# A decoder trunk with split fp32 weights: another order of the work between its two layers, and two other reckoned times in its planner

## The chip, the cores and the metric

The kernel runs on one core of a Trainium2 chip. The metric is device time in microseconds (us), lower is better. The engines are called as the profile calls them: PE (TensorE, the matrix engine), ACT (ScalarE), DVE (VectorE), POOL (GpSimd) and SP (SyncE, which here only issues transfers).

## The reference

`h` has 256 tokens of 1024 features in fp32. Two layers each do

```python
h = h + 0.5 * swiglu(rmsnorm(h, ffn1_norm), ffn1_w_gate, ffn1_w_up, ffn1_w_down)   # D_FF = 2752
u = rmsnorm(h, mix_norm); z = u @ w_in        # gated mLSTM and sliding-window attention
h = h + 0.5 * (sigmoid(gA) * (A @ W_A) + sigmoid(gB) * (B @ W_B)) @ w_out
h = h + 0.5 * swiglu(rmsnorm(h, ffn2_norm), ffn2_w_gate, ffn2_w_up, ffn2_w_down)
h = h + sigmoid(rmsnorm(h, ple_norm) @ ple_gate_w) * (p[i] @ ple_proj_w)           # p[i]: 256 x 256
```

`rmsnorm` needs the whole row of a token, so nothing of a block's first matmul can start for a token before the block ahead has finished that token.

## The kernel before, in words

**Tiles and parts.** The 256 tokens are two token tiles of 128, t0 and t1 (`NT` = 2). Every fp32 weight W is split into a rounded high half `wh` and a rest `wl`, and activations likewise, so each product is three matmuls (`mm3`): x-high by `wh`, x-high by `wl`, x-low by `wh`. Weights come from HBM into one of two 1 MB buffers `raw`; each holds two parts of 128 x 1024. A part is split by a cast on ACT (`wh<-raw`) and a subtraction on DVE (`wl<-raw,wh`). The split parts go into a ring of eight. A `raw` buffer can be loaded again when the `wl` of its second part is done.

**The planner.** All work is written out in one program by a planner that keeps a reckoned time for each engine (class `Clock`); the engines then run their instructions in the order written. Before each pair of matmul groups `tick` advances chains of work whose reckoned time has come, and calls `feed`, which splits the next part if the reckoned times of ACT, DVE and of the part's arrival allow it. `Clock.DMA` is a fixed latency and a time per MB, from which `load` reckons arrivals. `store` counts parts split and not yet used; with `haste` set, `feed` splits no further part once `store` has reached `HASTE` = 3, so that DVE and ACT are free for the norm at a block's end. If a matmul needs a part that isn't split, `need` splits it then and there.

**The end of a block.** `project` runs a matmul over eight parts (two units n = 0, 1 of four parts) for both token tiles. With `first` = 3 and `last` = 5 the first three parts run for t0, then for t1, and the last five for t0, then for t1, so t0 ends 30 matmuls before t1. When an accumulator (n, t) is complete, `use` is deferred as a chain: in `ple` it is a tanh on ACT (`sg<-pg`), a DVE operation with `pp` (`sg<-sg,pp`), and `then`, which adds to `h` on DVE, takes the sum of squares on ACT (`sq<-h`) and, at n = 1, starts `norm`: `ms` on DVE, a power `r` on POOL, two `xn` on DVE, eight transposes on PE (`tp<-ident,xn`), and their copies `uT` (high on ACT, low on DVE). `haste` is set in `project` at the item `hurry` and cleared when t0's `norm` has issued its transposes.

**The blocks** are, per layer, ffn1, mix, ffn2, ple. A feed-forward block begins with `by_token`, whose matmuls the trace calls `gu`; in layer 1's ffn1 the first six parts run for t0 (36 matmuls) and then for t1. Its product `sg<-sg,gu` on DVE is transposed on PE (`tp<-ident,sg`). Further columns are `pg` and `pu`, the output `dn`. In `ple` the gate's matmul is `pg` too.

**The embeddings.** `prelude` of `ple` runs when ffn2's `dn` begins: SP issues the load of `p`, and `later_T` lets the planner place the transposes `tp<-ident,p` at a reckoned 5.0 us later. Their results are used by `pp`, after all of `dn`.

Of the kernel before, what the change touches and what calls it, by code (L numbers as in the profile page):

```python
# [22 lines left out]
NT = T // P  # L23
KT = D // P
DEPTH = 2
# [10 lines left out]
STORE, HASTE = 4, 3  # L36
# [9 lines left out]
def half(n):  # L46
    return slice(n * NB, (n + 1) * NB)


class Part:  # L50


    def __init__(self, c0, k, n):
        self.c0, self.k, self.n = c0, k, n
        self.hi = self.lo = self.ready = None
        self.fresh = True
        self.rows = None


class Clock:  # L60
# [5 lines left out]
    SYNC = 0.1  # L66
    TABLE = 1.4
    SETS = {AF.Silu: {0}, AF.Exp: {1}, AF.Tanh: {0, 1}, AF.Ln: {2}}
    DMA = (1.0, 2.9)

    def __init__(self):
        self.t = dict.fromkeys(self.COST, 0.0)
# [34 lines left out]
    def load(self, ready, mb=1.0):  # L107

        latency, per = self.DMA
        self.dma = max(self.dma, ready, self.now) + mb * per  # L110
# [53 lines left out]
class Trunk:  # L164
# [7 lines left out]
    def __init__(self, ctx, tc, a, out):  # L172
        self.tc, self.a, self.out = tc, a, out
        self.clock = Clock()
        self.nc = Core(self.clock, tc.nc)
        pool = lambda name, bufs, **k: ctx.enter_context(tc.tile_pool(name=name, bufs=bufs, **k))
        self.const = pool("const", 1)
        self.rawp = pool("raw", RAW)
        self.wp = pool("w", RING)
        self.slots = pool("slots", 22)  # L180
        self.gp = pool("g", 1)
        self.sc = pool("sc", 7)
        self.small = pool("small", 6)
        self.psum = pool("psum", 8, space=PSUM)
        self.n = 0
        self.jobs, self.bg, self.haste, self.entry = [], [], False, None
        self.pending, self.loaded, self.store = deque(), deque(), 0
        self.free, self.raws = deque([0.0] * RING), deque([0.0] * RAW)
        self.consts()
# [138 lines left out]
    def feed(self, must=False):  # L328

        clock = self.clock  # L330
        if not self.loaded or not self.free:
            return
        raw, parts = self.loaded[0]
        part, arrival = parts[0]
        slack = AHEAD[self.store >= STORE]
        if not must and max(self.free[0], arrival, clock.t["scalar"] - slack, clock.t["vector"] - slack) > clock.now:
            return
        if not must and self.haste and self.store >= HASTE:
            return
        self.store += 1  # L340
        ready = max(self.free.popleft(), arrival)
        parts.popleft()
        last = not parts
        if last:
            self.loaded.popleft()
        w = part.k * part.n
        hi = self.wp.tile([P, QU], F32R, tag="wh", name=self.name("wh"))[:, :w]
        lo = self.wp.tile([P, QU], F32R, tag="wl", name=self.name("wl"))[:, :w]

        def chain():  # L350
            src = raw[:, part.c0 : part.c0 + w]
            if part.rows is None:
                yield from self.splitting(hi, lo, src)
            else:
                self.tc.nc.gpsimd.memset(lo[part.rows.stop :].bitcast(F32), 0.0)
                self.nc.scalar.copy(hi, src)
                yield
                r = part.rows
                self.nc.vector.tensor_tensor(lo[r], src[r], hi[r].bitcast(F32), op=ALU.subtract)
            part.ready = clock.done()  # L360
            if last:
                self.raws.append(part.ready)
                self.prefetch()

        part.hi, part.lo = (x.rearrange("p (k n) -> p k n", k=part.k) for x in (hi, lo))
        part.chain = self.later(chain())
        self.entry = self.entry or part.chain
        outer = clock.begin(dma=ready)
        self.advance(part.chain)
        clock.end(outer)  # L370
# [20 lines left out]
        mm(ps, xh, wl, start=False, stop=False, **kw)  # L391
        mm(ps, xl, wh, start=False, stop=stop, **kw)

    def project(self, units, xT, base, use, first=0, last=0):


        units = [[(sum(q.k for q in unit[:i]), part) for i, part in enumerate(unit)] for unit in units]
        todo = [(n, k0, part) for n, unit in enumerate(units) for k0, part in unit]
        cut = len(todo) - last
        apart = lambda items: [(x, t) for t in range(NT) for x in items]  # L400
        order = apart(todo[:first]) + [(x, t) for x in todo[first:cut] for t in range(NT)] + apart(todo[cut:])
        hurry = order[-last - 1] if last else None
        uses = {id(part): NT for _, _, part in todo}
        ps = {}
        for (n, k0, part), t in order:
            if ((n, k0, part), t) == hurry:
                self.haste = True
            if k0 == 0:
                ps[n, t] = None
            tok = slice(t * P, (t + 1) * P)  # L410
            for k in range(part.k):
                kk = k0 + k
                self.tick()
                xT.wait(kk, t)
                self.need(part)
                if ps[n, t] is None:
                    ps[n, t] = self.bank(base)[:, : part.n]
                self.mm3(ps[n, t], xT[0](kk, tok), xT[1](kk, tok), part.hi[:, k, :], part.lo[:, k, :], kk == 0,
                         kk == KT - 1)
            uses[id(part)] -= 1  # L420
            if not uses[id(part)]:
                self.drop(part)
            if kk == KT - 1:
                self.defer(use, n, t, ps[n, t])
# [94 lines left out]
    def norm(self, t, ss, g, xT):  # L519

        nc = self.nc
        ms, r = self.col("ms"), self.col("r")
        nc.vector.scalar_tensor_tensor(ms, ss[:, 0:1], EPS, ss[:, 1:2], op0=ALU.add, op1=ALU.add)
        self.power(r, ms)
        yield
        xn = []
        for n in range(2):
            xn.append(self.scr("xn"))
            nc.vector.scalar_tensor_tensor(xn[n], self.h[t][:, half(n)], r, g[n], op0=ALU.mult, op1=ALU.mult)
        yield  # L530
        for n in range(2):
            self.to_T(xn[n], xT, n * 4, t)
        if t == 0:
            self.haste = False

    def first_norm(self, t, g, xT):

        ss = self.col("ss", 2)
        for n in range(2):
            self.sumsq(t, n, ss)  # L540
        yield
        norm = self.norm(t, ss, g, xT)
        yield next(norm)
        yield next(norm)
        if t == 0 and self.entry is not None:
            self.advance(self.entry)
        yield from norm
# [133 lines left out]
    def ple(self, l, xT, sink):  # L681


        nc, a = self.nc, self.a
        prepare, then = sink
        pT = self.new_T("pT", 2)
        pp = []
        wp = self.columns(a["ple_proj_w"][l].rearrange("(k p) n -> p k n", p=P))
        wg = self.pair(a["ple_gate_w"][l], 0)

        def run():
            prepare()
            ps = {(t, n): self.bank("pp") for t in range(NT) for n in range(2)}
            for k in range(2):
                for t in range(NT):
                    self.tick()
                    self.need(wp[k])
                    pT.wait(k, t)
                    tok = slice(t * P, (t + 1) * P)
                    for n in range(2):  # L700
                        s = half(n)
                        self.mm3(ps[t, n], pT[0](k, tok), pT[1](k, tok), wp[k].hi[:, 0, s], wp[k].lo[:, 0, s],
                                 k == 0, k == 1)
                self.drop(wp[k])
            for t in range(NT):
                pp.append(self.slot("pp"))
                for n in range(2):
                    nc.scalar.copy(pp[t][:, n * NB : (n + 1) * NB], ps[t, n])

            def use(n, t, ps):  # L710
                sg = self.scr("sg")
                nc.scalar.activation(sg, ps, AF.Tanh, scale=0.5)
                nc.vector.scalar_tensor_tensor(sg, sg, 1.0, pp[t][:, n * NB : (n + 1) * NB], op0=ALU.add, op1=ALU.mult)
                then(n, t, sg)
            self.project(wg, xT, "pg", use, first=3, last=5)
        self.jobs.append(run)

        def prelude():
            p = self.slot("p")[:, : NT * 2 * P].rearrange("p (t n) -> p t n", t=NT)
            nc.sync.dma_start(p, a["p"][l, 0].rearrange("(t p) n -> p t n", p=P))  # L720
            for t in range(NT):
                self.later_T(p[:, t, :], pT, 0, t, 2, self.clock.now + 5.0)
        return prelude


# [552 lines left out]
```

## Time and profile before

| | |
|---|---|
| median of 3 runs | 1404.9 us (1402.35 to 1405.91) |
| the profiled execution | 1401.73 us |
| its span in the profile | 1400.0 us |
| PE busy | 1384.3 us (99%) |
| DVE, ACT busy | 863.0 us (62%), 727.8 us (52%) |
| transfers | 243.81 MB, mean 174 GB/s |

The profile shows one execution; the span runs from its first to its last instruction. "Busy" counts a PE at half its clock as busy too, so the windows view, which gives the granted clock (PEclk, 1.00 is full), is needed beside it. Nearly all instructions are issued in one helper, line L130, so groups are told apart by the names of their operands. L324 is the load of a `raw`, L498 that of a norm's gain, L720 that of `p`.

### The profile page before, as it was taken

How to read it: one execution, taken by the hardware profiler on the slowest of the kernel's cores; microseconds unless marked ns; L12 is line 12 of the kernel's file. 1: busy time of each engine (PE TensorE's matmuls, PEld its weight loads, DVE VectorE, ACT ScalarE, POOL GpSimd, SP SyncE). 2: the span in 40 equal slices, each digit the busy share in tenths (PEclk: the TensorE clock that was granted, in tenths of full speed). 3: DMA queues.
4: the chain of work that ended last, by engine and by line, in shares of the span. 5: the costliest groups of instructions: out<-in, count | busy, mean ns of one | idle time of the engine just before them, and what ended most of it. 6: DMA issues, size and time to landing. Idle time of an engine off the chain costs nothing.

```text
span 1400.0 us, 21954 instructions
## 1 busy us (share of the span) xinstructions
PE 1384.3 (99%) x9056; PEld 1249.0 (89%) x9056; DVE 863.0 (62%) x1213; ACT 727.8 (52%) x1138; POOL 53.8 (4%) x84
## 2 busy tenths in 40 slices
PE   8999999999999999999999999999999999999998
PEld 6999887899899889988879998878998998999886
DVE  5655457656886665454565554586668876554544
ACT  5554346765665454443554443467656654444433
POOL 0000012000000000000000000120000000000000
PEclk9999999999999999999999999999999999999999
DMA  6665645355545565565456566443545544755651
GB/s 210 221 206 172 219 147 182 107 135 169 177 151 181 166 204 188 166 232 181 149 172 210 178 198 212 143 145 117 151 151 196 175 158 161 220 190 182 203 180 60
DMA packets 125830, 243.81 MB, mean 174 GB/s; under 512 B 14977, under 2 KB 23841, under 8 KB 125730
## 3 DMA queue, kind: packets, MB, share of 16 engines
q1 hardware_dynamic: 125730, 242.41, 54.2%
q8 instruction: 71, 1.16, 0.3%
q14 instruction: 29, 0.24, 0.1%
HBM read 241.34 MB, written 1.05 MB: 173 GB/s over the span
## 4 chain that ended last, share of the span: by engine, by line
PE 93%; DMA 3%; DVE 2%; ACT 1%; issue 1%; POOL 0%; SPq 0%; ACTq 0%; POOLq 0%
PE dn L130 16%; PE pg L130 15%; PE pu L130 14%; PE gt L130 7%; PE z L130 7%; PE gu L130 6%; PE kvq L130 5%; PE ya L130 3%; PE v L130 3%; PE ym L130 3%; PE og L130 3%; PE yo L130 3%; PE tp L130 3%; PE sc L130 2%; DMA raw<-in_ffn_w_gate_dram 1%; PE ha L130 1%
## 5 line engine op out<-in xcount | busy, mean ns | idle before, releaser
L130 DVE TENSOR_TENSOR wl<-raw,wh 128x1024 fp32r<-128x1024 f32 (+1 forms) x448 | 541.5, 1222 | 372.8 <-ACT wh L130 369.3
L130 ACT CAST wh<-raw 128x1024 fp32r<-128x1024 f32 x448 | 461.8, 1049 | 432.7 <-PE dn L130 88.4
L130 PE MATMUL dn<-wh,hid 128*128 128x512 f32 x688 | 217.9, 395 | 0.0
L130 PE MATMUL pg<-uT,wh 128*128 128x256 f32 x1088 | 194.6, 282 | 0.0
L130 PE MATMUL pu<-uT,wh 128*128 128x256 f32 x1088 | 193.6, 281 | 0.0
L130 PEld LDWEIGHTS pg<-uT,wh 128*128 128x128 f32 x1088 | 167.1, 189 | 0.2
L130 PEld LDWEIGHTS pu<-uT,wh 128*128 128x128 f32 x1088 | 166.9, 189 | 0.0
L130 PEld LDWEIGHTS dn<-wh,hid 128*128 128x128 f32 x688 | 129.3, 188 | 29.8
L130 PE MATMUL pg<-uT,wl 128*128 128x256 f32 x544 | 153.2, 282 | 0.0
L130 PE MATMUL pu<-uT,wl 128*128 128x256 f32 x544 | 153.1, 281 | 0.0
L130 PE MATMUL dn<-wl,hid 128*128 128x512 f32 x352 | 139.1, 395 | 0.0
L130 PEld LDWEIGHTS pu<-uT,wl 128*128 128x128 f32 x544 | 102.7, 189 | 0.0
L130 PEld LDWEIGHTS pg<-uT,wl 128*128 128x128 f32 x544 | 102.6, 189 | 0.0
L130 PE MATMUL gt<-uT,wh 128*128 128x256 f32 x512 | 93.7, 284 | 0.0
L130 PE MATMUL z<-uT,wh 128*128 128x256 f32 x512 | 92.3, 282 | 0.0
L130 PE MATMUL gu<-wh,uT 128*128 128x512 f32 x256 | 84.3, 406 | 1.2 <-ACT uT L130 1.2
L130 PEld LDWEIGHTS gt<-uT,wh 128*128 128x128 f32 x512 | 79.0, 189 | 1.2
L130 PEld LDWEIGHTS dn<-wl,hid 128*128 128x128 f32 x352 | 66.2, 188 | 15.1
L130 PEld LDWEIGHTS z<-uT,wh 128*128 128x128 f32 x512 | 78.7, 189 | 0.2
L130 PE MATMUL z<-uT,wl 128*128 128x256 f32 x256 | 72.1, 282 | 0.0
L130 PE MATMUL gt<-uT,wl 128*128 128x256 f32 x256 | 72.0, 281 | 0.0
L130 PE MATMUL kvq<-wh,uT 128*128 128x512 f32 x192 | 63.7, 402 | 0.0
(194 smaller groups left out, 2061.5 us busy)
## 6 DMA issues: line engine op xcount, KB each, us to landing
raw<-in_w_in_dram SPq DMA_DIRECT2D x60, 1024.0 KB, 5.1
raw<-in_ffn_w_up_dram SPq DMA_DIRECT2D x40, 1024.0 KB, 5.1
raw<-in_ffn_w_down_dram SPq DMA_DIRECT2D x40, 1024.0 KB, 5.2
raw<-in_ffn_w_gate_dram SPq DMA_DIRECT2D x39, 1024.0 KB, 5.7
raw<-in_w_branch_a_dram SPq DMA_DIRECT2D x16, 512.0 KB, 6.0
raw<-in_w_branch_m_dram SPq DMA_DIRECT2D x8, 1024.0 KB, 5.0
raw<-in_w_out_dram SPq DMA_DIRECT2D x8, 1024.0 KB, 5.1
raw<-in_ple_gate_w_dram SPq DMA_DIRECT2D x8, 1024.0 KB, 6.6
```

Source lines behind the costliest of these rows:

```text
L130: return issue(*args, **kw)
```

## The change

It consists of four edits.

1. `Clock.DMA`'s latency is 2.0 us in place of 1.0.
2. In `ple` of layer 0, `use` for t1 (both units) doesn't issue its tanh until `normed` says that t0's norm of this block has issued its two `xn`.
3. `project` has an argument `early`; `ple` passes 3, which sets `haste` three items sooner, and then `feed` stops at a store of `suffices` = 1 in place of 3. Both are set back when t0's norm has issued its transposes.
4. The transposes of `p` are placed at a reckoned 15.0 us after the load's issue in place of 5.0.

```diff
-    DMA = (1.0, 2.9)
+    DMA = (2.0, 2.9)
...
-        self.jobs, self.bg, self.haste, self.entry = [], [], False, None
+        self.jobs, self.bg, self.haste, self.entry, self.normed = [], [], False, None, 0
+        self.suffices = HASTE
...
-        if not must and self.haste and self.store >= HASTE:
+        if not must and self.haste and self.store >= self.suffices:
             return
...
-    def project(self, units, xT, base, use, first=0, last=0):
+    def project(self, units, xT, base, use, first=0, last=0, early=0):
...
-        hurry = order[-last - 1] if last else None
+        hurry = order[-last - 1 - early] if last else None
...
             if ((n, k0, part), t) == hurry:
-                self.haste = True
+                self.haste, self.suffices = True, 1 if early else HASTE
...
+        if t == 0:
+            self.normed += 1
         yield
         for n in range(2):
             self.to_T(xn[n], xT, n * 4, t)
         if t == 0:
-            self.haste = False
+            self.haste, self.suffices = False, HASTE
...
                 sg = self.scr("sg")
+                while t == NT - 1 and l < DEPTH - 1 and self.normed <= 4 * (l + 1):
+                    yield
                 nc.scalar.activation(sg, ps, AF.Tanh, scale=0.5)
...
-            self.project(wg, xT, "pg", use, first=3, last=5)
+            self.project(wg, xT, "pg", use, first=3, last=5, early=3)
...
-                self.later_T(p[:, t, :], pT, 0, t, 2, self.clock.now + 5.0)
+                self.later_T(p[:, t, :], pT, 0, t, 2, self.clock.now + 15.0)
```

Since the planner decides the order, the edits move instructions in many places. Some of them follow, from three places. Numbers behind a name count buffers and tiles and differ between the two kernels.

**Between the layers, DVE.** These are DVE's instructions from the end of t0's last `pg` to the first copies `uT` of layer 1's ffn1. `h_88` and `pp_6904` belong to t0, `h_89` and `pp_6907` to t1; `raw_6942` and the `raw` after it hold the first parts of layer 1's ffn1. Before:

```order
L130 TENSOR_TENSOR wl_6983<-raw_6942,wh_6982 128x1024
L130 TENSOR_TENSOR wl_7007<-raw_6942,wh_7006 128x1024
L130 TENSOR_TENSOR wl_7013<-raw_6968,wh_7012 128x1024
L130 SCALAR_TENSOR_TENSOR sg_7031<-sg_7031,pp_6904 128x512
L130 SCALAR_TENSOR_TENSOR h_88<-sg_7031,h_88 128x512
L130 SCALAR_TENSOR_TENSOR ms_7037<-ss_6992 128x1
L130 SCALAR_TENSOR_TENSOR sg_7047<-sg_7047,pp_6907 128x512
L130 SCALAR_TENSOR_TENSOR h_89<-sg_7047,h_89 128x512
L130 SCALAR_TENSOR_TENSOR xn_7064<-h_88,r_7038,g_6853 128x512
L130 SCALAR_TENSOR_TENSOR xn_7066<-h_88,r_7038,g_6853 128x512
L130 TENSOR_TENSOR uT_166<-tp_7077,uT_164 128x4x128
L130 TENSOR_TENSOR uT_167<-tp_7084,uT_165 128x4x128
```

After:

```order
L130 SCALAR_TENSOR_TENSOR ms_7026<-ss_6989 128x1
L130 TENSOR_TENSOR wl_7015<-raw_6942,wh_7014 128x1024
L130 SCALAR_TENSOR_TENSOR xn_7048<-h_88,r_7027,g_6853 128x512
L130 SCALAR_TENSOR_TENSOR xn_7050<-h_88,r_7027,g_6853 128x512
L130 SCALAR_TENSOR_TENSOR sg_7037<-sg_7037,pp_6907 128x512
L130 SCALAR_TENSOR_TENSOR h_89<-sg_7037,h_89 128x512
L130 TENSOR_TENSOR uT_166<-tp_7067,uT_164 128x4x128
L130 TENSOR_TENSOR uT_167<-tp_7074,uT_165 128x4x128
L130 SCALAR_TENSOR_TENSOR sg_7093<-sg_7093,pp_6907 128x512
L130 SCALAR_TENSOR_TENSOR h_89<-sg_7093,h_89 128x512
L130 SCALAR_TENSOR_TENSOR ms_7099<-ss_7055 128x1
L130 TENSOR_TENSOR wl_7082<-raw_6942,wh_7081 128x1024
```

Three `wl` stood ahead of t0's second `sg` and its `ms`; now one stands between `ms` and `xn`, none ahead. The next two `wl` come behind t1's second `ms_7099`, as two came before (`wl_7092` is next in the kernel before), and t1's first `sg` comes behind t0's `xn`. ACT's casts move with them.

**Between the layers, PE.** These rows end the first part of layer 1's first `gu` and begin the second. Before, and then after:

```order
L130 MATMUL gu_7113<-wh_6982,uT_166 128x512
L130 MATMUL gu_7113<-wh_7006,uT_164 128x512
L130 MATMUL gu_7113<-wl_7007,uT_164 128x512
L130 MATMUL gu_7113<-wh_7006,uT_166 128x512
L130 MATMUL gu_7113<-wh_7006,uT_164 128x512
```

```order
L130 MATMUL gu_7103<-wh_7014,uT_166 128x512
L130 MATMUL gu_7103<-wh_7081,uT_164 128x512
L130 MATMUL gu_7103<-wl_7082,uT_164 128x512
L130 MATMUL gu_7103<-wh_7081,uT_166 128x512
L130 MATMUL gu_7103<-wh_7081,uT_164 128x512
```

The place in PE's order is the same; the second part was one of those split ahead (`wl_7007`), and is now `wl_7082`, which on DVE stands behind `ms_7099`. PE's transposes of t0's norm keep their place too, 18 matmuls into t1's last unit.

**At 510 us of the trace, the first steps of layer 0's ffn2, DVE.** `sg_5223` is t0's product, which PE transposes, and `raw_5265` (before) or `raw_5271` (after) the buffer that a load of `in_ffn_w_up` fills. Before, and then after:

```order
L130 TENSOR_TENSOR wl_5276<-raw_5221,wh_5275 128x1024
L130 TENSOR_TENSOR wl_5283<-raw_5221,wh_5282 128x1024
L130 TENSOR_TENSOR wl_5308<-raw_5265,wh_5307 128x1024
L130 TENSOR_TENSOR sg_5223<-sg_5223,gu_5225 128x512
L130 TENSOR_TENSOR wl_5314<-raw_5265,wh_5313 128x1024
L130 TENSOR_TENSOR sg_5273<-sg_5273,gu_5278 128x512
```

```order
L130 TENSOR_TENSOR wl_5280<-raw_5221,wh_5279 128x1024
L130 TENSOR_TENSOR wl_5286<-raw_5221,wh_5285 128x1024
L130 TENSOR_TENSOR sg_5223<-sg_5223,gu_5225 128x512
L130 TENSOR_TENSOR wl_5318<-raw_5271,wh_5317 128x1024
L130 TENSOR_TENSOR sg_5273<-sg_5273,gu_5275 128x512
L130 TENSOR_TENSOR wl_5324<-raw_5271,wh_5323 128x1024
```

`sg_5223` moves ahead of the first `wl` of that buffer.

**At ffn2's `dn`, PE.** The rows around the transposes of layer 0's `p`. Before, and then after:

```order
L130 MATMUL dn_6444<-wl_6265,hid_152 128x512
L130 MATMUL dn_6444<-wh_6264,hid_158 128x512
L130 MATMUL tp_6482<-ident,p_6439 128x128 x2
L130 MATMUL tp_6485<-ident,p_6439 128x128 x2
L130 MATMUL dn_6441<-wh_6307,hid_152 128x512
L130 MATMUL dn_6441<-wl_6308,hid_152 128x512
```

```order
L130 MATMUL dn_6438<-wl_6406,hid_153 128x512
L130 MATMUL dn_6438<-wh_6405,hid_159 128x512
L130 MATMUL tp_6546<-ident,p_6433 128x128 x2
L130 MATMUL tp_6549<-ident,p_6433 128x128 x2
L130 MATMUL dn_6435<-wh_6449,hid_153 128x512
L130 MATMUL dn_6435<-wl_6450,hid_153 128x512
```

Before, 24 matmuls of `dn` stand ahead of the transposes, after, 72, in both layers.

## Rows read from the trace of the kernel before

**Rows 1.** The page, part 1: busy time, share of the span, instructions.

```profile
PE 1384.3 (99%) x9056; PEld 1249.0 (89%) x9056; DVE 863.0 (62%) x1213; ACT 727.8 (52%) x1138; POOL 53.8 (4%) x84
```

**Rows 2.** The page, part 4: the chain that ended last, by engine.

```profile
PE 93%; DMA 3%; DVE 2%; ACT 1%; issue 1%; POOL 0%; SPq 0%; ACTq 0%; POOLq 0%
```

**Rows 3.** Waits of TensorE: us in total, times, longest us.

```profile
PE tp L130 <- DVE xn L130: 4.0, 2, 2.5
...
PE tp L130 <- DVE wl L130: 1.6, 1, 1.6
...
PE tp L130 <- DVE sg L130: 1.0, 1, 1.0
```

**Rows 4.** Windows: us, busy PE, PEld, DVE, ACT, POOL; PEclk, DMA share, GB/s.

```profile
700.30:702.80 2.50, 0.02 (x2) 0.01 (x1) 2.15 (x5) 1.01 (x3) 0.55 (x1) 1.00 0.45 174
...
702.80:706.50 3.70, 3.70 (x14) 3.17 (x15) 1.98 (x3) 2.47 (x5) 0.00 (x0) 0.54 0.02 4
...
706.50:720.00 13.50, 13.50 (x63) 10.83 (x62) 9.93 (x12) 6.51 (x11) 1.46 (x1) 1.00 0.48 155
```

**Rows 5.** TensorE timeline between the layers: start us, us, what, [idle before].

```profile
694.33 0.63 PE L130 MATMUL pg<-wh,uT 128*128 128x512 f32 x2
...
699.92 0.40 PE L130 MATMUL pg<-wh,uT 128*128 128x512 f32 x1
...
702.79 1.82 PE L130 MATMUL tp<-ident,xn 128*128 128x128 f32 x8 [2.48 <-DVE xn L130]
...
706.71 0.40 PE L130 MATMUL gu<-wh,uT 128*128 128x512 f32 x1
...
715.90 0.63 PE L130 MATMUL gu<-wh,uT 128*128 128x512 f32 x2
```

**Rows 6.** ScalarE timeline between the layers.

```profile
703.79 0.58 ACT L130 CAST uT<-tp 128x512 fp32r<-128x512 f32 x1 [0.96 <-PE tp L130]
...
705.13 2.00 ACT L130 CAST wh<-raw 128x1024 fp32r<-128x1024 f32 x2
...
707.02 0.60 ACT L130 ACTIVATE sg<-pg 128x512 f32<-128x512 f32 x1
...
709.10 0.63 ACT L130 ACTIVATE sq<-h 128x512 f32<-128x512 f32 x1 [1.48 <-DVE h L130]
```

**Rows 7.** VectorE timeline between the layers.

```profile
707.65 0.69 DVE L130 SCALAR_TENSOR_TENSOR sg<-sg,pp 128x512 f32<-128x512 f32 x1 [1.70 <-ACT sg L130]
...
709.86 0.16 DVE L130 SCALAR_TENSOR_TENSOR ms<-ss 128x1 f32<-128x1 f32 x1 [0.79 <-ACT sq L130]
...
709.93 2.35 DVE L130 TENSOR_TENSOR wl<-raw,wh 128x1024 fp32r<-128x1024 f32 x2
...
712.21 1.41 DVE L130 SCALAR_TENSOR_TENSOR xn<-h,r,g 128x512 f32<-128x512 f32 x2
```

**Rows 8.** GpSimd timeline between the layers.

```profile
710.10 1.46 POOL L130 TENSOR_TENSOR r<-ms,mhalf 128x1 f32<-128x1 f32 x1 [9.14 <-DVE ms L130]
```

**Rows 9.** The page, part 6: transfers, KB each, median us from issue to landing.

```profile
raw<-in_ffn_w_up_dram SPq DMA_DIRECT2D x40, 1024.0 KB, 5.1
```

**Rows 10.** Chain that ended last, 688 to 720 us: start us, us.

```profile
683.40 7.47 DMA raw<-in_ffn_w_gate_dram
```

**Rows 11.** Timeline at 510 us, VectorE and TensorE.

```profile
509.38 1.22 DVE L130 TENSOR_TENSOR wl<-raw,wh 128x1024 fp32r<-128x1024 f32 x1 [4.17 <-ACT wh L130]
...
510.52 0.68 DVE L130 TENSOR_TENSOR sg<-sg,gu 128x512 f32<-128x512 f32 x1
...
511.26 0.66 PE L130 MATMUL tp<-ident,sg 128*128 128x128 f32 x4 [1.04 <-DVE sg L130]
```

**Rows 12.** Timeline at 616 us, TensorE.

```profile
616.74 0.63 PE L130 MATMUL tp<-ident,p 128*128 128x128 f32 x4 [0.33 <-DMA p<-in_p_dram]
```

**Rows 13.** Timeline at 1308 us, SyncE queue and TensorE.

```profile
1303.65 0.38 SPq L720 DMA_DIRECT2D p<-in_p_dram  x1
...
1309.98 0.63 PE L130 MATMUL tp<-ident,p 128*128 128x128 f32 x4 [1.65 <-DVE wl L130]
```

## The prediction

> **What bounds the kernel now.** I read the page first. PE is busy in 99% of the span [rows 1], and the chain that ended last is PE for 93% [rows 2]. So PE sets the time: DVE and ACT matter only where PE waits for them, and all that PE doesn't do in 1400.0 us is 1400.0 − 1384.3 = 15.7 us. No reordering can win more than that, apart from time at a lowered clock.
>
> The waits of PE [rows 3] say where these are. The longest, 2.5 us, is transposes `tp` waiting for `xn`: t0's norm between the layers. The timeline there [rows 5] shows `tp` at 702.79 after 2.48 us of idleness. The windows [rows 4] show what follows: from 702.80 to 706.50 PE counts as fully busy, but the granted clock is 0.54, that is near the lower of its levels (1.2 and 2.4 GHz), where it was 1.00 ahead; from 706.50 it is 1.00 again. Of these 3.70 us 46%, 1.7 us, are lost too. The place costs 2.5 + 1.7 = 4.2 us and a few tenths.
>
> Two more waits of PE are in reach of the change. At 510 us `tp<-ident,sg` idles for 1.04 us behind DVE's `sg`, which started at 510.52 because it stood in DVE's queue behind a `wl` begun at 509.38 after 4.17 us of idleness [rows 11]. At 616 us and 1308 us the transposes of `p` idle for 0.33 us [rows 12] and 1.65 us [rows 13]. The second is put down to a `wl`, but it starts 6.3 us after SP issued the load of `p` (1303.65 to 1309.98), the operand is `p`, and at 616 us the same instruction is put down to that load; I read both as the load.
>
> **The change part by part.** The DMA figure and the place of `p`'s transposes add no instruction. Where `p` is transposed 72 instead of 24 matmuls into `dn`, PE comes there 48 matmuls later. From t1's `pg`, 24 of which take 699.92 − 694.33 = 5.59 us [rows 5], one takes 0.233 us, so 11.2 us later: past the 6.3 us of the load. Both waits go: −0.3 and −1.65. What `p` feeds comes after all of `dn`, so nothing is late by it. At 510 us DVE's `sg` now stands ahead of the `wl` that waits for its transfer, so −1.0. If PE gains nothing at these places the sum loses 3.0; it can't gain more than idles there. A `wl` that starts later at 510 us has as cover the three parts split ahead of it.
>
> Between the layers the change takes two casts and two `wl` from ahead of t0's norm and puts t1's tanh behind it. I follow it in the new order with the durations of before, taking the start of the next matmul after t0's last as 694.33 + 0.23 = 694.56.
>
> 1. t0's last `pg` ends near 694.7, its tanh starts near 694.9. The steps that follow are those of t1's second unit: tanh to DVE `sg` 0.63 (707.02 to 707.65), to `sq` 1.45 more (709.10), to `ms` 0.76 more (709.86) [rows 6, 7]. So `ms` starts at 697.7. One `wl`, 1.2 us [rows 7, 11], follows it, to 699.0; POOL's `r` lies beside it (0.55 us in [rows 4], 1.46 in [rows 8]; it is ready at 698.5 or 699.4). The two `xn`, 1.41 us [rows 7], end at 700.4 or 700.8.
> 2. PE comes to the transposes after 24 matmuls of t1, at 694.56 + 5.59 = 700.15, just when the first `xn` is done. **The 2.48 us and the half clock behind them are gone.** Eight transposes, about 0.8 us (half of the 1.82 at half clock [rows 5]), and six matmuls, 1.4: `pg` ends at 702.35.
> 3. What is late next: t1's first `sg` stands on DVE behind `xn`, starts at 700.4, and its `sq` on ACT 1.45 later at 701.85; `uT` stands behind it on ACT, begins near 702.6 and takes 0.58 us [rows 6]. So `gu` starts at 703.2, 0.9 us late, and its third matmul, which reads DVE's low `uT`, waits another 0.3.
> 4. Only one part is split ahead, where three were. The second part's cast and another follow `uT` on ACT, 2.0 us [rows 6], to 705.65; only then t1's second tanh, and 2.84 us after it (707.02 to 709.86, as in step 1) `ms` at 708.5. The second part's `wl` stands on DVE behind that `ms`, so it ends at 708.55 + 1.2 = 709.75. PE wants it at 703.2 + 0.3 + 7 × 0.233 = 705.1. **A new wait of 4.6 us.**
> 5. Behind it DVE has another `wl` (to 710.95), t1's two `xn` (712.35), the fourth part's `wl` (713.55). PE does the rest of parts two and three, 11 matmuls, by 712.4 and waits 0.9 us for that.
> 6. The buffer of parts one and two is free only at 709.75, so the load for part five is issued then, and lands at 5.1 us [rows 9], 714.9. ACT copies t1's `uT` until about 715.5, then casts part five until 716.5; its `wl` ends near 717.75, that of part six near 719.4. Part six's last five matmuls then end at 720.6, where t1's `gu` begins.
>
> Before, t1's `gu` began at 715.90 + 0.23 = 716.13 [rows 5]: 36 matmuls and eight transposes after 706.71, as counted here. So the place costs **+4.5 us**, the won wait and clock already in it. Here an idle PE of 2.48 us was followed by half clock [rows 4, 5]; I take it that 4.6 us will be too. From 709.75 PE would then be slowed for about 3.7 us, but it has only 12 matmuls, 2.8 us, before the wait of step 5: at half clock eight of them fit, and the rest end 0.7 us later. I add 0.7: **+5.2**. Ends of the range: +3.8 (no half clock, a step or two shorter) and +8.2 (a late load, below).
>
> The Trainium skill, page "TensorE: Matmul & The Clock Gate", section "HAM oscillation — how this bites in real kernels", prices time at the low clock by that time times one half, whatever the engine would have waited for. By it the 3.7 us would cost 1.85 instead of 0.7 us, an estimate, and the sum would be 1.1 us higher; no row here has a wait right behind a half-clock stretch that would decide it.
>
> Sum: against the profiled execution's span, 1400.0 − 1.0 − 0.3 − 1.65 + 5.2 = 1402.2, so the execution 1401.7 + 2.2 = 1403.9. It lies 3.2 us under the median of the runs, to which the same difference is added: 1404.9 + 2.2 = **1407 us**.
>
> **The rivals.** *A: the place is cured.* If PE doesn't wait for the second part's `wl` or the later ones, only the 1.2 us of step 3 stay: t1's `gu` begins at 702.35 + 1.2 + 36 × 0.233 + 0.8 = 712.7, 3.4 us earlier than before. With −3.0 elsewhere the median is 1398.5, faster. For it: 2.5 us and a clock loss are there to be won, and steps 1 and 2 win them. Against it: `wl` behind `ms` in DVE's order, and at 709.86 and 709.93 the rows show just this, a `wl` starting 0.07 us after an `ms` that it had stood behind [rows 7]. The Trainium skill, page "PSUM — Partial Sum Buffer", section "Engine vs sequencer instructions", calls VectorE's queue strictly first in, first out; by that rule A can't happen with this order, and the trace agrees (the 0.07 us).
>
> *B: a late load, slower.* The load of part five is on the path now. One load of the same kind took 7.47 us [rows 10]. Then it lands at 717.2, part five's `wl` ends near 719.6, t1's `gu` begins near 722.5 (+6.4), and PE, idle for most of 713 to 719.6, falls to half clock again at up to 1.8 us: +8.2, the median 1404.9 − 3.0 + 8.2 = 1410. It decides for slower when the place costs over 7.2 us. For it: little work is left to fill the queue. Against it: the median of the 40 loads is 5.1, and when this one is issued both buffers are otherwise full, so it has the engines to itself, as in the window with a share of 0.02 [rows 4].
>
> *C: the three small gains don't come*, because in each place something else is late, too: 1404.9 + 5.2 = 1410, at the bound of slower.
>
> **How the numbers follow.** The likeliest case, 0.55: 1404 to 1409 by the ends 1404.9 − 3.0 + 3.8 and + 7. A 0.20, B 0.17, C 0.08 (half of it beyond the bound). A measurement can tell about 0.3%, 4.2 us, from no change: faster is under 1400.7, slower over 1409.1. Faster 0.20 (A), same 0.55 + 0.04 = 0.59, slower 0.17 + 0.04 = 0.21. The range runs from A's 1398 to just over B and C, 1411; what is left out is waits that the new order opens elsewhere.
>
> **What would show it.** Right: in the waits of PE no `tp` behind `xn` between the layers, no `tp` behind `sg` at 510 us, no waits at the transposes of `p`; and new waits of `gu` for `wl`, one above 4 us, then one or two of about 1 us, with a window of half clock after the first; SP's load of `in_ffn_w_up` issued near 710 us. Wrong: a `gu` that runs through its first parts (A), a load of 7 us there (B), the old waits still there (C), or an idle of PE above 1 us at a place not named here, in the attention of layer 0 above all, where ACT's order changes most.

## The result, and the profile after

The changed kernel takes 1407.22 us (median of 22 runs, 1405.62 to 1410.88), the kernel before, run beside it, 1405.41 us (22 runs, 1399.91 to 1409.99). The ratio is 1.0025, 95% interval 1.0014 to 1.0036: a little slower, and within the 0.3% that the prediction called no change. The profiled execution took 1406.94 us, its span is 1405.2 us, 5.2 us longer than before's. That is more than the 1.8 us between the medians, because executions of either kernel differ in how often PE's clock is halved in the attention (last section), and before's profile is one of those without it.

The page of the changed kernel, parts 1 and 4:

```profile
PE 1386.6 (99%) x9056; PEld 1248.0 (89%) x9056; DVE 859.4 (61%) x1213; ACT 721.9 (51%) x1138; POOL 64.5 (5%) x84
...
PE 97%; ACT 1%; DVE 1%; DMA 0%; issue 0%; POOL 0%; SPq 0%; ACTq 0%
```

PE is still busy for 99% and the chain is now PE for 97% [rows 1, 2]. The waits of PE in the changed kernel:

```profile
PE gu L130 <- DVE wl L130: 5.7, 3, 4.3
...
PE gu L130 <- ACT uT L130: 1.8, 2, 1.2
...
PE gu L130 <- ACT wh L130: 1.0, 1, 1.0
...
PE if L130 <- DVE wif L130: 0.8, 1, 0.8
```

The wait of `tp` for `xn` between the layers is gone, as are those of `tp` for `sg` and at the transposes of `p` [rows 3, 11, 12, 13]. `gu` waits instead, and the longest of its waits, 4.3 us, is for a `wl`. Where it lies is in PE's timeline between the layers:

```profile
700.73 1.32 PE L130 MATMUL tp<-ident,xn 128*128 128x128 f32 x8
...
703.95 0.51 PE L130 MATMUL gu<-wh,uT 128*128 128x512 f32 x1 [0.51 <-ACT uT L130]
...
710.36 0.50 PE L130 MATMUL gu<-wl,uT 128*128 128x512 f32 x1 [4.26 <-DVE wl L130]
...
717.99 0.50 PE L130 MATMUL gu<-wh,uT 128*128 128x512 f32 x1 [0.98 <-ACT wh L130]
...
719.25 0.50 PE L130 MATMUL gu<-wl,uT 128*128 128x512 f32 x1 [0.76 <-DVE wl L130]
...
721.72 0.63 PE L130 MATMUL gu<-wh,uT 128*128 128x512 f32 x2
```

The transposes start at 700.73 with no idle ahead. `gu` starts at 703.95, and after seven matmuls its next stands at 710.36 behind 4.26 us of idleness. Part five starts at 717.99 and has two more waits. t1's `gu` is the second matmul of the last row, at 721.95 (716.13 before [rows 5]). ACT, then DVE, then SP's queue tell why:

```profile
703.33 1.05 ACT L130 CAST uT<-tp 128x512 fp32r<-128x512 f32 x2
...
704.27 2.00 ACT L130 CAST wh<-raw 128x1024 fp32r<-128x1024 f32 x2
...
706.17 0.60 ACT L130 ACTIVATE sg<-pg 128x512 f32<-128x512 f32 x1
```

```profile
698.18 0.16 DVE L130 SCALAR_TENSOR_TENSOR ms<-ss 128x1 f32<-128x1 f32 x1 [0.79 <-ACT sq L130]
...
699.92 1.41 DVE L130 SCALAR_TENSOR_TENSOR xn<-h,r,g 128x512 f32<-128x512 f32 x2 [0.44 <-POOL r L130]
...
709.01 0.16 DVE L130 SCALAR_TENSOR_TENSOR ms<-ss 128x1 f32<-128x1 f32 x1 [0.79 <-ACT sq L130]
...
709.09 2.35 DVE L130 TENSOR_TENSOR wl<-raw,wh 128x1024 fp32r<-128x1024 f32 x2
```

```profile
710.37 3.93 SPq L325 DMA_DIRECT2D raw<-in_ffn_w_up_dram  x2
```

On ACT two casts `wh` (704.27) stand between `uT` and t1's second tanh (706.17). On DVE `ms` follows at 709.01, and only then, 0.08 us later, two `wl`, for the first of which `gu` waits. The load for part five is issued at 710.37, when the first of them is done. The windows (us, busy PE, PEld, DVE, ACT, POOL; PEclk, DMA share, GB/s) show the clock:

```profile
705.00:710.30 5.30, 1.10 (x5) 0.57 (x3) 2.89 (x6) 3.43 (x6) 1.05 (x1) 1.00 0.00 0
...
710.30:714.30 4.00, 3.94 (x10) 3.10 (x11) 3.60 (x5) 0.00 (x0) 0.41 (x1) 0.58 0.67 201
...
714.30:718.00 3.70, 2.72 (x17) 2.00 (x15) 1.32 (x3) 2.08 (x4) 0.00 (x0) 0.99 0.95 311
...
932.80:936.20 3.40, 3.40 (x11) 2.74 (x11) 2.87 (x6) 0.52 (x1) 0.00 (x0) 0.50 0.02 5
```

After the long wait the granted clock is 0.58 over 4.0 us; after the wait in the kernel before it was 0.54 over 3.7 us [rows 4]. The last row is another place, 932.8 us, in layer 1's attention: PE has no idle time there or ahead of it, and the clock is at the lower level all the same.

Where the 5.2 us come from is read from the starts of the same matmuls in both traces. I take the place between the layers from the 337th `dn` (629.26 us before, in layer 0's ffn2) to the 289th `gu` (718.97, in t1's first parts of layer 1): 89.71 us before.

| stretch | changed against before |
|---|---|
| start to layer 0's `kvq` (198.62) | +0.25 |
| to layer 0's `ym` (its 49th matmul, 445.58) | +1.77 |
| to ffn2's `pg` (514.32): the wait at 510 us | −1.17 |
| to the 337th `dn`: transposes of `p` | −0.54 |
| to the 289th `gu`: between the layers | **+5.47** |
| to layer 1's `kvq` (891.47) | −0.59 |
| to layer 1's `ym` (1131.48) | +1.67 |
| to layer 1's `dn` (1324.42): transposes of `p` | −1.88 |
| to the end | about +0.2 |

The −0.59 in layer 1 stands in e5, which has edit 4 alone, too (−0.54); what it comes from was not followed up.

### The profile page after: what moved, and what is told of

It is laid out like the page before. It is cut to its first block, busy times and chain, and to the rows that moved or that the text cites. A ratio compares the mean times of both kernels' runs of the same rounds, so it can differ in the third digit from the quotient of the medians.

```text
span 1405.2 us, 21882 instructions
## 1 busy us (share of the span) xinstructions
PE 1386.6 (99%) x9056; PEld 1248.0 (89%) x9056; DVE 859.4 (61%) x1213; ACT 721.9 (51%) x1138; POOL 64.5 (5%) x84
## 4 chain that ended last, share of the span: by engine, by line
PE 97%; ACT 1%; DVE 1%; DMA 0%; issue 0%; POOL 0%; SPq 0%; ACTq 0%
PE dn L130 17%; PE pg L130 16%; PE pu L130 14%; PE gu L130 7%; PE gt L130 7%; PE z L130 6%; PE kvq L130 5%; PE ya L130 3%; PE ym L130 3%; PE og L130 3%; PE yo L130 3%; PE v L130 3%; PE tp L130 3%; PE sc L130 2%; PE ha L130 1%; PE pp L130 1%
```

## The experiments

**Theory 1** is that of the prediction: the new cost lies between the layers and comes from edit 3, which leaves one part split ahead, so the next parts' `wl` come behind t1's `ms`. **Theory 2** is the rival that edit 2, the held-back tanh, costs it. Each kernel was timed beside the kernel before; "place" is the stretch from the 337th `dn` to the 289th `gu` in its trace, against before's 89.71 us. The places are compared rather than the medians, which a halved clock in the attention can move by 4 us.

| run | edits in it | place, us | median, us | ratio to before (95%) |
|---|---|---|---|---|
| changed kernel | 1, 2, 3, 4 | +5.47 | 1407.22 | 1.0025 (1.0014 to 1.0036) |
| e1_noearly | 1, 2, 4 | +0.72 | 1401.38 | 0.9997 (0.9983 to 1.0010) |
| e2_noyield | 1, 3, 4 | +3.22 | 1405.39 | 1.0020 (1.0006 to 1.0034) |
| e3_store2 | all, store 2 | +3.13 | 1404.20 | 1.0000 (0.9988 to 1.0013) |
| e4_dma1 | 2, 3, 4 | +5.39 | 1404.22 | 1.0014 (1.0000 to 1.0028) |
| e5_p_only | 4 | −0.03 | 1398.97 | 0.9959 (0.9940 to 0.9977) |
| e6_yield_p | 2, 4 | +0.20 | 1403.19 | 0.9993 (0.9973 to 1.0012) |
| e7_last7_yield | 2, 4, more cover | +0.19 | 1400.77 | 0.9971 (0.9960 to 0.9983) |
| e8_last6_noyield | 4, more cover | −0.27 | 1402.63 | 0.9982 (0.9964 to 1.0001) |
| e9_dma_only | 1 | −0.27 | 1401.13 | 0.9971 (0.9953 to 0.9990) |
| e10_fill | all, PE kept busy | +6.25 | 1407.95 | 1.0018 (1.0000 to 1.0035) |
| e11_dma_p | 1, 4 | −1.52 | 1401.33 | 0.9976 (0.9957 to 0.9996) |
| e12_early_only | 3 | +4.97 | 1406.49 | 1.0021 (1.0002 to 1.0040) |

**e1_noearly: without edit 3.**

```diff
-            self.project(wg, xT, "pg", use, first=3, last=5, early=3)
+            self.project(wg, xT, "pg", use, first=3, last=5)
```

> The changed kernel with edit 3 left out (project in ple gets no early argument, so haste comes at the old item and three parts may be stored); edits 1, 2 and 4 stay. Theory 1 (the new cost between the layers comes from edit 3: one part split ahead, the second part's wl behind ms): the 4.3 us wait of gu for wl goes; three parts are ready when gu begins, one wait of about 2 us for the fourth part's wl stays, the load of in_ffn_w_up is issued some 10 us earlier, and t1's gu begins about 5.8 us earlier relative to t0's last pg than in the changed kernel; 4 to 6 us faster than the changed kernel, 1401 to 1404 us, ratio to before 0.997 to 1.000. Theory 2 (the cost comes from edit 2, t1's tanh held back): the waits of gu stay above 4 us in all and the time within 1.5 us of the changed kernel, 1406 to 1409 us.

Waits of PE (the other 1.2 us of the first row are at the kernel's start):

```profile
PE tp L130 <- DVE xn L130: 3.0, 2, 1.8
...
PE gu L130 <- DVE wl L130: 1.7, 2, 1.0
```

The place falls from +5.47 to +0.72, by 4.75 us (5.8 expected), the long wait is gone, and the load of `in_ffn_w_up` is issued at 696.71. What I hadn't expected is that `tp` waits for `xn` again, for 1.8 us: ACT's third cast waits 1.23 us for its load ahead of t0's second tanh, and the half clock follows there. Theory 1 holds; theory 2 alone can't.

**e2_noyield: without edit 2.**

```diff
-                while t == NT - 1 and l < DEPTH - 1 and self.normed <= 4 * (l + 1):
-                    yield
```

> The changed kernel with edit 2 left out (t1's tanh is not held back); edits 1, 3 and 4 stay. Theory 1: the second part's wl still stands behind t1's second ms on DVE, so a wait of gu for wl of 3.5 to 4.5 us stays and the time is within 2 us of the changed kernel, 1405 to 1409 us. Theory 2: the wait goes with the yield, and the time is 3 us or more below the changed kernel, 1404 us or less.

```profile
PE gu L130 <- DVE wl L130: 2.7, 4, 0.9
...
PE gu L130 <- ACT wh L130: 2.4, 1, 2.4
```

The place costs 3.22, so edit 2 has a share: 2.25 us come and go with it. The wait for the second part is now 2.4 us for its cast `wh`, which stands behind t1's `sq` on ACT, and 0.8 for its `wl`, so it is one wait of 3.2 us in two pieces, just under what I expected. Theory 2, that the wait goes with edit 2, is wrong; that edit 2 adds nothing is wrong as well.

**e3_store2: a store of 2 in place of 1.**

```diff
-                self.haste, self.suffices = True, 1 if early else HASTE
+                self.haste, self.suffices = True, 2 if early else HASTE
```

> The changed kernel with a store of 2 in place of 1 under early; all else stays. Theory 1: two parts are ready, the buffer of parts one and two is freed before gu begins, and only the third part's wl stands behind ms: the long wait shrinks from 4.3 to about 3.2 us, the waits of about 1 us for part five go, t1's gu begins about 4 us earlier than in the changed kernel, the time is 2 to 5 us below the changed kernel, between it and the run with edit 3 left out. Theory 2: no change beyond 1.5 us against the changed kernel.

```profile
PE gu L130 <- DVE wl L130: 4.3, 3, 2.9
```

The longest wait is 2.9 us, the load for part five is issued at 699.96, no wait for a cast is left, but there is one of 1.0 us for part six's `wl`, and the place costs 3.13, 2.3 us less than with a store of 1. It lies between e1 and the changed kernel, as theory 1 has it; the gain is smaller than the 4 us I gave.

**e4_dma1: without edit 1.**

```diff
-    DMA = (2.0, 2.9)
+    DMA = (1.0, 2.9)
```

> The changed kernel with edit 1 undone (the reckoned latency of a transfer 1.0 again); edits 2 to 4 stay. Between the layers the order has the same parts behind ms, so both theories expect the long wait of gu, 4 to 4.5 us, to stay. What it tells apart is where the rest comes from: if edit 1 brought the gain at 510 us, the wait of tp for sg is back at about 1.0 us (+1.2); if it brought the new wait at the gates matmul if (0.8 us for wif) and the small ones in layer 0's attention, these go (-1.5 to -2). Sum about -0.5 against the changed kernel: 1405 to 1409 us. If the gain at 510 us came from something else, the wait of tp for sg stays away.

```profile
PE gu L130 <- DVE wl L130: 5.4, 3, 4.3
...
PE tp L130 <- DVE sg L130: 0.9, 1, 0.9
```

The place stays at +5.39, the wait at 510 us is back (0.9), and the wait of `if` is gone. So edit 1 is what won at 510 us and what lost in layer 0's attention. The waits at `p` stay away without edit 1.

**e9_dma_only: edit 1 alone** (the kernel before with the line of e4 the other way round).

> The kernel before with edit 1 alone (latency 2.0). Theory 1: edit 1 brings the gain at 510 us (no wait of tp for sg, 1.2 us start-to-start) and, not foreseen in the prediction, new waits in layer 0's attention (if for wif 0.8 us, and small ones: about 2.0 us by the stage of ym); the waits of tp for p stay (0.3 to 1.7 us). Between the layers three parts are ready and no wait of gu for wl above 2.5 us. In executions without a half-clock stretch in the attention about +0.5 to +1.5 us against before, ratio 1.000 to 1.002. Rival: the waits in the attention belong to the other edits; then no wait of if, and a gain of 1 us or more.

```profile
PE if L130 <- DVE wif L130: 0.8, 1, 0.8
```

SP's load of `p` and PE's transposes of it:

```profile
611.12 0.43 SPq L724 DMA_DIRECT2D p<-in_p_dram  x1
...
621.09 0.60 PE L130 MATMUL tp<-ident,p 128*128 128x128 f32 x4
```

No wait of `tp` for `sg` in this list, and that of `if` is there: both belong to edit 1. A miss: the waits at `p`, expected to stay, are gone as well. Their transposes stand behind 24 matmuls of `dn` as in the kernel before, but SP issues the load 10.0 us ahead of them instead of 6.2 (at 1308 us 10.0 instead of 6.3), so edit 1 alone wins what edit 4 alone wins: 0.58 and 2.02 us here, 0.49 and 1.77 in e5. Up to `ym` the trace is 6.09 us late, but 4.1 of this is a half clock of 10.2 us in the attention that the changed kernel's profile doesn't have (2.02); of the other 2.0, some 1.8 lie in the attention and are edit 1's. The ratio, 0.9971, is below the 1.000 to 1.002 expected. Executions alike in mean granted clock say the same: at 0.998 the median of six is 1401.1 us, that of four of before beside it 1402.2, so it is some 1 us ahead where 0.5 to 1.5 behind was expected; the 2.6 us of gains at `p` account for the difference.

**e12_early_only: edit 3 alone** (edits 1, 2 and 4 undone).

> The kernel before with edit 3 alone (haste three items sooner, a store of 1). Theory 1: edit 3 suffices for the new cost: the second part's wl stands behind t1's second ms, gu waits for it 3 to 4.5 us, the load of in_ffn_w_up is issued only then, the place costs 3 to 5.5 us more than before; nothing is gained elsewhere, so 3 to 5.5 us slower than before, ratio 1.002 to 1.004. Theory 2 (it is edit 2 or both together): no wait of gu above 2 us and the place within 1.5 us of before.

```profile
PE gu L130 <- DVE wl L130: 4.9, 3, 3.6
...
PE tp L130 <- DMA p<-in_p_dram: 0.8, 1, 0.8
```

Edit 3 alone costs 4.97 us here, nearly the 5.47 of all four. The waits at `p` are there (0.8 us, and 1.7 at 1308 us), with neither edit 1 nor edit 4.

The places of the runs add up. Edit 3 costs 4.75 us (changed kernel against e1) or 4.74 (e2 against e11) where edit 1 is in, 5.19 (e4 against e6) or 4.97 (this run) where it isn't. Edit 2 costs 2.25 us (changed kernel against e2) or 2.24 (e1 against e11) where edit 1 is in, with edit 3 or without it, and only 0.4 (e4 against this run, which has no edit 4) or 0.2 (e6 against e5) where it isn't. So the 5.47 are 4.75 of edit 3, 2.24 of edit 2 and −1.52 of edits 1 and 4. Why edit 2 costs more with edit 1 was not followed up.

**e5_p_only and e6_yield_p: edit 4 alone, and with edit 2.**

> The kernel before with edit 4 alone (the transposes of p at a reckoned 15 us). Theory 1: the two waits of tp for p go and nothing else moves: the place between the layers and the wait at 510 us stay as before, the stretch of the trace about 1308 us gains 1.8 us of start-to-start time and that about 616 us 0.5, together 2.3 us, ratio to before 0.9984, 1402.5 to 1403.5 us where before is 1405. Rival: what p feeds comes late (waits of pp for pT), then 0.5 us or less are won.

```profile
PE tp L130 <- DVE xn L130: 4.0, 2, 2.5
...
PE tp L130 <- DVE sg L130: 1.0, 1, 1.0
```

Waits at `p` are gone, those of `xn` (2.5 us at this place) and `sg` as before. By 1324.42 us the trace is 2.42 us ahead: the two gains of 0.5 and 1.8. The measured ratio, 0.9959, is better than the 0.9984 expected from these; six of its eight executions had no long half clock (mean clock of 0.998 or more), of before's 32 beside it 12. It has the lowest median of all versions measured, with the single line of edit 4.

> Edits 2 and 4 alone (t1's tanh held back; p at 15 us; the store stays 3, the latency 1.0). Three wl stand ahead of t0's second sg as before. Theory 1: what held t0's norm were those three and POOL's power, not t1's tanh: tp waits for xn for 1.4 to 2.3 us (2.5 before), uT and t1's norm come 0.8 to 1.6 us later than before, so the fourth part's wl too, and t1's gu begins 0 to 1.6 us later than before; with p's 2.3 the sum is -2.3 to -0.7, ratio 0.9984 to 0.9995. Theory 2 (the held-back tanh is what decides, for good here): the wait of tp for xn falls under 0.5 us, no half clock follows, t1's gu begins 3 us or more earlier than before, sum -5 or better, ratio 0.9965 or less.

```profile
PE tp L130 <- DVE xn L130: 2.9, 2, 1.5
...
PE gu L130 <- DVE wl L130: 2.3, 2, 1.5
```

`tp` waits 1.5 us for `xn` (2.5 before) and no half clock follows, but the fourth part's `wl` is waited for 1.5 us: what is won ahead is given back, place +0.20, as theory 1 had it.

**e7_last7_yield and e8_last6_noyield: more cover for t0's norm**, in the kernel with edits 2 and 4, and with edit 4.

```diff
-            self.project(wg, xT, "pg", use, first=3, last=5)
+            self.project(wg, xT, "pg", use, first=1, last=7)
```

> Edits 2 and 4 with more cover instead of fewer parts: in ple first=1, last=7, so t0's last pg ends 42 matmuls ahead of t1's in place of 30; latency 1.0, store 3. Theory 1 (t0's norm needs cover on PE, and the parts must be split ahead of t1's norm, not behind it): wl of parts four and five stand ahead of t1's second ms, no wait of gu for wl above 0.5 us, tp waits for xn for 0 to 1.5 us and no half clock follows; t1's gu begins 2 to 4.5 us earlier than before; with p's 2.3 the sum is -4 to -6.5, ratio 0.9955 to 0.997. Rival: ple's own last parts, needed 2.8 us sooner by t0, come late from HBM and split: waits of pg for wl of 2 us or more ahead, ratio 0.998 to 1.000.

```profile
PE tp L130 <- DVE xn L130: 4.6, 3, 1.8
```

A miss: the place costs +0.19, where −2 to −4.5 was expected. Its waits for `xn` are three, two of them here, 1.3 us of t0's and 1.8 of t1's norm, which now comes behind the parts. Cover for one norm seems to have been taken from the other; no run here tells that from other causes.

> Edit 4, and first=2, last=6 in ple: t0's last pg ends 36 matmuls ahead of t1's; no yield, latency 1.0, store 3. Theory 1: t1's first sg and h still stand ahead of xn, and a wl too, so tp waits for xn for about 1 us; with its six matmuls more of cover t1's gu begins 0 to 2 us earlier than before; with p's 2.3 the sum is -2.3 to -4.3, ratio 0.997 to 0.9985, behind the run with last=7 and the yield. Theory 2 (the yield is harmful in itself): it is ahead of that run.

The place is −0.27 us, within the range given, and no worse than e7's +0.19: the held-back tanh of edit 2 isn't needed for it. Its median is above e7's, but eight of its twelve executions have, by their mean clock, a half clock in the attention (last section).

**e10_fill: PE kept busy in the wait.**

```diff
+                if base == "gu" and t == 0 and (n, k0, k) == (0, part.k, 0):
+                    self.gus = getattr(self, "gus", 0) + 1
+                    if self.gus == 3:
+                        fill = self.bank("fill")
+                        for _ in range(17):
+                            self.tc.nc.tensor.matmul(fill, xT[0](kk, tok), part.hi[:, k, :], start=True, stop=True)
                 self.mm3(ps[n, t], xT[0](kk, tok), xT[1](kk, tok), part.hi[:, k, :], part.lo[:, k, :], kk == 0,
```

> The changed kernel with 17 matmuls more, whose results nobody reads, put into PE's queue between the layers ahead of the second part's first matmul, in the time in which PE waits for that part's wl. The output stays the reference's. The wait itself stays, but PE isn't idle in it. What it measures is the price of the half clock after the wait. The prediction's: the granted clock stays 1.00 there and t1's gu begins 0.7 us earlier than in the changed kernel (up to 1.1). By half of the stretch: 1.7 to 1.85 us earlier. If the clock falls all the same, or if the waits for part five swallow it all: 0 to 0.2.

PE's timeline, and windows:

```profile
703.45 0.50 PE L130 MATMUL gu<-wh,uT 128*128 128x512 f32 x1 [0.51 <-ACT uT L130]
...
705.21 4.13 PE L425 MATMUL fill<-wh,uT 128*128 128x512 f32 x17
...
709.86 0.50 PE L130 MATMUL gu<-wl,uT 128*128 128x512 f32 x1 [0.30 <-DVE wl L130]
...
716.74 0.50 PE L130 MATMUL gu<-wh,uT 128*128 128x512 f32 x1 [0.98 <-ACT wh L130]
```

```profile
702.30:709.80 7.50, 6.75 (x27) 4.55 (x25) 3.96 (x7) 5.64 (x10) 1.04 (x1) 1.00 0.01 2
...
709.80:715.30 5.50, 4.90 (x24) 3.84 (x25) 3.62 (x6) 0.63 (x2) 0.42 (x1) 1.00 0.72 204
...
718.10:721.50 3.40, 3.40 (x8) 2.67 (x9) 3.19 (x3) 2.00 (x3) 0.00 (x0) 0.50 0.26 42
```

The clock stays 1.00 through the wait, in which the unread matmuls `fill` run, and behind it. From `gu`'s start to part five's are 716.74 − 703.45 = 13.29 us, in the changed kernel 717.99 − 703.95 = 14.04: **the half clock after the wait costs 0.75 us**, the prediction's 0.7. But then the clock falls at 718.1, behind the waits for part five, in front of work that waits for nothing, and takes back more than was won: place +6.25, and t1's `gu` begins not 0.7 us earlier after `gu`'s start, as expected, but 0.8 later (18.8 against 18.0 us). In that window 8 matmuls took 3.4 us, at 0.233 us each they would take 1.9.

**e11_dma_p: without edits 2 and 3.**

> The changed kernel without edits 2 and 3, so edits 1 and 4. Theory 1: without edit 3 the parts are ready and the place between the layers costs within 1.5 us of before; the gains at 510, 616 and 1308 us (3.5) stand against 2.0 in layer 0's attention: 0 to 3 us faster than before, 4 to 6 us faster than the changed kernel in executions alike in the attention's clock. Theory 2 (edit 1 or 4 itself costs the 4 us): within 1.5 us of the changed kernel.

PE between the layers:

```profile
706.32 1.03 PE L130 MATMUL tp<-ident,xn 128*128 128x128 f32 x8
...
707.59 0.50 PE L130 MATMUL gu<-wh,uT 128*128 128x512 f32 x1 [0.24 <-ACT uT L130]
```

The place is −1.52 us, the best of all runs: theory 2 in the form that edit 1 or 4 costs the 4 us is wrong. The transposes start without a wait for `xn` here too, though neither edit that aims at this wait is in: in this order they stand behind all of t1's `pg`, six matmuls later than in the changed kernel, and no long wait of `gu` follows. Its profile has 17 us of half clock in the attention, so the profiled time says less than the place. Alike in clock (0.998) three of its executions have a median of 1400.8 us, where before's four have 1402.2.

## Why the prediction was right, step by step

*1 and 2, t0's norm.* Right. `ms` was put at 697.7 and came at 698.18, `xn` at 699.0 and came at 699.92 (POOL's power took 1.47 us, the upper bound), the transposes at 700.15 and came at 700.73, without a wait. PE is 0.52 us late on entering this place (its last `pg` ahead of the transposes starts at 700.44, before at 699.92 [rows 5]), which accounts for most of the differences.

*3, the next thing late.* Right: `gu` was put at 703.2 and came at 703.95; 0.5 us of idleness stand in its row, where 0.9 was expected.

*4, the second part's `wl` behind `ms`.* Right in place and size: `ms` at 708.5 (709.01), a wait of 4.6 us (4.26). What the prediction didn't work out is how the edits share it: e12 shows edit 3 alone at +4.97; in the changed kernel 4.75 us are edit 3's and 2.24 edit 2's, and −1.52 that of edits 1 and 4, which e11 shows to end the wait for `xn` without the other two.

*5 and 6, the later parts.* Right: the load issued at 709.75 (710.37), part five's cast done at 716.5 without half clock, 717.2 with it (PE starts it at 717.99), t1's `gu` at 720.6 + 0.7 = 721.3 (721.95). The place was put at +5.2, and is +5.47. The half clock's 0.7 us was shown by e10 to be 0.75. The Trainium skill's rule (page "TensorE: Matmul & The Clock Gate", section "HAM oscillation — how this bites in real kernels"), half of the low-clock time, would have made it 1.85, an estimate from the prediction's 3.7 us. The measurement decides against it here, where waits follow that swallow most of it, and is near it where none follow: 3.4 − 1.9 = 1.5 of 3.4 us in e10's window.

*The gains at 510, 616 and 1308 us.* Right in place and slightly too small: 3.0 expected from the idle times, 1.17 + 0.54 + 1.88 = 3.59 found from start to start. That the place of the transposes of `p` brings the second and third is only half of it: with edit 1 the load is issued early enough by itself (e9), so either edit suffices (edit 4 alone in e5), and with both the gain is no larger than with edit 1 alone.

*What was missed.* Two terms. Edit 1 costs about 1.8 us in layer 0's attention. The matmul `if` waits 0.76 us for `wif`, whose cast stands on ACT behind one more cast of weights than before (e4 and e9 tie it to edit 1); the other 1 us is spread over small pieces:

```profile
311.19 1.05 ACT L130 CAST wh<-raw 128x1024 fp32r<-128x1024 f32 x1
312.13 0.34 ACT L130 CAST wif<-wif 128x32 fp32r<-128x32 f32 x2
...
312.84 1.42 PE L130 MATMUL if<-uT,wif 128*128 128x256 f32 x10 [0.76 <-DVE wif L130]
```

And 1.67 us come from the half clock at 932.8 us, which no row of before announced; in e1, which doesn't have it, the same stretch is +0.04. With both, the profiles differ by 5.2 us where the sum said 2.2. That the median came out at 1407.2 all the same, 1.8 us above before's, fits executions of before that were slowed in the attention more often: 14 of its 22 lie above 1403.5 us, while of the changed kernel's 22 only six lie above 1408.3. Executions alike in the attention can be compared by their mean clock. Those of before beside e1 have a median of 1401.6 us (seven) at 0.999 and of 1406.3 (eight) at 0.995; the changed kernel's 22 have 1406.1 (ten) at 0.997, its two short stretches in it, and 1410.6 (six) at 0.993. Compared so, it is 4.3 to 4.5 us slower. So the step that failed is that layer 0's attention was put at nothing, where it cost 1.8 us, beside the half clock that wasn't foreseen; the close agreement of the total is partly luck. The lower end of the likeliest case is also mis-added: 1404.9 − 3.0 + 3.8 is 1405.7, not 1404.

*The rivals.* A (cured) falls with the order on DVE: `wl` 0.08 us behind `ms`. B (a late load) didn't happen. C (no gains) is wrong in all three places.

## What to carry to other kernels

When work is moved out of the way of one chain on an in-order engine, look at what it stands behind now: the parts that weren't split ahead of t0's norm were split behind t1's, and holding the splits back cost 4.7 to 5.2 us at that place in each of the four pairs of runs that show it. Look, too, whether the stall needs a cure of its own: two changed figures in the planner ended it here (e11). A stall of half clock costs only what later waits don't swallow, so price it against the next wait, not by its length. And a planner's reckoned figure is an edit of the whole program: read the order at every place where an engine has little slack, not only where the change is aimed.

## What the runs showed of the hardware

The granted clock falls to the lower level in the attention of either layer although PE isn't idle. Windows of e8_last6_noyield, which had it in both layers:

```profile
232.00:236.90 4.90, 4.90 (x35) 3.93 (x33) 3.86 (x7) 2.28 (x4) 1.64 (x1) 1.00 0.60 190
...
236.90:247.10 10.20, 10.20 (x30) 7.31 (x30) 5.27 (x13) 7.74 (x29) 1.36 (x1) 0.50 0.04 14
...
929.00:933.30 4.30, 4.30 (x31) 3.39 (x29) 2.38 (x5) 1.64 (x3) 1.64 (x1) 0.99 0.63 236
...
933.30:943.50 10.20, 10.20 (x28) 7.29 (x29) 5.53 (x14) 7.74 (x29) 1.91 (x9) 0.50 0.00 0
```

What PE did just ahead of the first:

```profile
233.92 1.55 PE L130 MATMUL sc<-kT,qT 64*128 64x128 f32 x12
...
235.72 1.75 PE L130 MATMUL sc<-kT,qT 64*128 64x128 f32 x12
```

Both stretches last about 10.2 us at 0.50, with PE busy throughout and ahead of them; what PE did just ahead were 24 matmuls `sc` of 64 rows among others of full size. In before's trace the same kind stands at 927.0 and 928.8 us and the clock stays at 1.00, so these matmuls alone don't decide it, and the cause stays open. It happens in some executions of a kernel and not in others: those of e8 lie at 1397.0 to 1398.9 us (mean clock 0.999, four), 1402.0 to 1403.7 (0.995 to 0.996, five) and 1407.7 to 1408.2 (0.992, three), so one stretch costs 4 to 5 us. Whether edit 1's order in the attention makes it rarer, as the fewer such executions of the changed kernel may suggest, wasn't settled. This scatter is larger than what most edits here are worth, and the comparison of the same stretch in two traces told more than 12 timed runs.
